# Reload tables in two buffers, a gated-attention branch begun three steps earlier, and a product block held behind the third pair of heads

## The chip, the cores and the metric

The kernel runs on one core of a Trainium2 chip. The metric is device time in microseconds (us), the median of several executions. All data are float32. The core has TensorE (PE, matrix products; its weight loads are listed apart as PEld), VectorE (DVE), ScalarE (ACT), GpSimd (POOL) and SyncE (SP), which here issues nearly all DMAs in one queue, in program order. Each engine runs its own instructions in a fixed order and waits on semaphores for the others.

## The reference

An encoder of two layers over 256 tokens of width 1024. Each layer is a half-step SwiGLU feed-forward block, a mixer and a second feed-forward block; the mixer is what the change touches:

```
h = RMSNorm(x)
u | q k v gate zf zb | aq ak av = split(h @ w_in)
y_s5   = S5(u)        # complex diagonal state space, both directions; gelu; y * sigmoid(y @ w_glu)
y_gla  = GLA(q,k,v,zf,zb): 4 heads, gated linear attention both ways,
         per-head RMSNorm, then * silu(gate)
y_attn = attention: 8 query heads, 2 key heads of 64, rotary, softmax
gates  = sigmoid(h @ w_merge_gate + b)       # 3 x 1024 columns
x += (gates0*(y_s5@w_s5) + gates1*(y_gla@w_gla) + gates2*(y_attn@w_attn)) @ w_out
```

## The kernel before, in words

**Dense products.** Every weight matrix is streamed once. `load` (L204) brings 128 x 2 x 512 blocks (512 KB) into a ring of five raw buffers, ScalarE rounds each into `hi` (L224), VectorE subtracts to get `lo` (L225), and `mm3` makes three products of 512 columns per pair of k-row and token tile (L234 to L236). A step of `stream` (L238) takes four k-rows, so 24 products. An optional `held` instruction makes the products of a block stand behind that instruction in the order (`behind`, L196); it is an ordering edge on TensorE's own queue and no semaphore.

**The mixer** (L671) is a main chain of steps into which three side generators are woven by `weave` (L94). The main chain is the input projection (blocks listed from L716, two steps each, the first two blocks together as steps 0 to 3, 14 steps in all) and then the parts of `MAIN` (L42): the three gate streams g0 to g2 (four steps each), `S` (what is left of S5), `G` (S5's GLU), `b0` (branch of S5), `L` (rest of GLA), `b10` (first half of GLA's branch), `A` (rest of attention), `b11`, `b20`, `b21`, and then the output product. `RATES` (L41) gives for S5, GLA and attention, in this order, the main step from which the generator is advanced and how many of its own steps it advances per main step. S5 has 34 own steps, GLA 27 (three for its gates, then six for each head), attention 19 (seven for norm and rotary, then three for each of four pairs of heads). What `weave` sets is the order in which instructions are emitted, with a priority for the sides; from it a planner with a cost model of its own fixes each engine's order of instructions and the hand-over of buffers.

**S5** (L778) runs in four quarters. For each quarter it needs tables that were computed ahead, during the feed-forward blocks, by `s5_tables` (L515): `bb` and `cc` (512 KB each), `e` (768 KB: 512 KB of turn factors and, behind them, 256 KB of decay factors `rr`), and `mt` (128 KB). Quarters 1 to 3 are stored to scratch memory (`scr`) and loaded back; quarter 0 stays where it was computed, and is the last to be computed. In a quarter: 8 products S from `bb` (L816; the trace has each as two passes), four VectorE products of `e` with S and two sums, four scans with `rr` (L833, L834), four more products of `e` with the scans' results, and 48 small products yp from `mt` and `cc` (L851, L854). `s5_tiles` (L770) has one buffer for each table, and all four loads stand at the head of the quarter that uses them, so that a load waits until the quarter before has used its table for the last time.

**GLA** (L921) computes its gate logits `lg` and decays for all heads, and then for each head cumulative sums, scores `sp`, states `kv`, output `go`, the norm and the product with the swish gate `gs`, and a transposition `goT`. `gs` is made by `ev_g` (L706) when the gate block of the input projection is complete. **Attention** (L1018) has for each pair of heads the scores `as` (L1068), a softmax, transpositions `apt` (L1083) and the products `ao` (L1090); then `split_into` makes hi and lo of the result. `self.last_ao` is the last `ao` product issued, and `b11` is held behind it (L736). S, yp, lg, sp, kv, go, as and ao all take PSUM tiles from one ring of three buffers (`psm`, L137).

Of the kernel before, what the change touches and what calls it, by code (L numbers as in the profile page):

```python
# [15 lines left out]
P = 128  # L16
# [12 lines left out]
NQ = 4  # L29
# [10 lines left out]
PREP = ((2, 1.8), (6, 0.85))  # L40
RATES = (3, 2.5, 10, 2.0, 14, 1.75)  # L41
MAIN = "g0 g1 g2 S G b0 L b10 A b11 b20 b21"  # L42
# [6 lines left out]
SCR_BB, SCR_CC, SCR_E, SCR_R, SCR_M, SCR = 0, 1024, 2048, 3072, 3584, 3840  # L49
SCR_AT = {"bb": (SCR_BB, SCR_CC), "e": (SCR_E, SCR_M), "cc": (SCR_CC, SCR_E), "mt": (SCR_M, SCR)}  # L50

# [74 lines left out]
class Enc:  # L126
# [388 lines left out]
    def s5_tables(self, l, pp):  # L515
# [38 lines left out]
        for q in (1, 2, 3, 0):  # L554
# [31 lines left out]
            for i in range(2):  # L586
                for a in range(4):
                    for d in range(2):
# [9 lines left out]
            v.scalar_tensor_tensor(ks[:, :, 3], dm, dcol, kp[0][:, :, 0], op0=ALU.mult, op1=ALU.add)  # L598
            E = ld["e"][:, :SCR_R - SCR_E].rearrange("p (r g c) -> p r g c", r=2, g=GQ)
            f8 = [self.ef[:, i, gs].unsqueeze(2).to_broadcast((P, GQ, 8, 8)) for i in range(2)]  # L600
# [3 lines left out]
            yield from self.cmul_steps(e8[0], e8[1], f8[0], f8[1], g8[0], g8[1], tt)  # L604
            nc.gpsimd.tensor_tensor(ld["e"][:, SCR_R - SCR_E:].rearrange("p (g c) -> p g c", g=GQ),
                                    self.r4[:, gs].unsqueeze(2).to_broadcast((P, GQ, 64)),
                                    self.tab(C_RM, 64).unsqueeze(1).to_broadcast((P, GQ, 64)), op=ALU.mult)
            scr = self.scr[l, q]
            if q:
                for name in ("bb", "cc", "e"):  # L610
                    a, z = SCR_AT[name]
                    nc.sync.dma_start(scr[:, a:z], ld[name])
# [58 lines left out]
    def mixer(self, l, nm, nxt):  # L671
        nc = self.nc
        with self.tc.tile_pool(name=f"mx{l}", bufs=1) as mp:
# [32 lines left out]
            def ev_g(t, ps):  # L706
# [13 lines left out]
                (cols((w, c(1024, 1536))), 512, ev_tr(m["kT"])),  # L720
                (cols((w, c(1536, 2048))), 512, self.evac_scaled(lambda t: m["v"][:, t], rstd)),
                (cols((w, c(2592, 3104))), 512,
                 self.evac_scaled(lambda t: m["qk"][:, t, 0:8].rearrange("p h d -> p (h d)"), rstd)),
                (cols((w, c(2048, 2560))), 512, ev_g),
            ]
# [43 lines left out]

    def s5_tiles(self):  # L770
        return {name: self.ld.tile([P, z - a], F32, name=self.nm(name), tag="s5" + name) for name, (a, z) in SCR_AT.items()}

# [5 lines left out]
    def s5(self, l, m):  # L778
# [20 lines left out]
        yield  # L799
        yg = mp.tile([P, 2, 4, 8, 16], F32, name=f"yg{l}", tag="yg")  # L800
        for q in range(NQ):
            if q:
                ld = self.s5_tiles()
                self.s5_load(l, q, ld, "bb", "e", "cc", "mt")
            else:
                ld = self.ahead.pop(l)
            bb = ld["bb"].rearrange("p (a r m) -> p a r m", a=4, r=2)
            e = ld["e"][:, :1024].rearrange("p (r c) -> p r c", r=2)
            rr = ld["e"][:, 1024:]
            cc = ld["cc"].rearrange("p (r g f) -> p r g f", r=2, g=GQ)  # L810
# [3 lines left out]
            for r in range(2):  # L814
                for a in range(4):
                    nc.tensor.matmul(S[r][:, a].rearrange("p g c -> p (g c)"), bb[:, a, r],  # L816
                                     U[:, pair[a]].rearrange("p g c -> p (g c)"), start=True, stop=True)
            yield
            t1, t2, t3, t4 = (self.t2([P, 512]) for _ in range(4))
# [12 lines left out]
            for i, V in ((0, t1), (1, t3)):  # L832
                nc.vector.tensor_tensor_scan(run[:64, i, 1:], rr[:64, :511], V[:64, :511], 0.0, op0=ALU.mult, op1=ALU.add)  # L833
                nc.vector.tensor_tensor_scan(run[64:, i, 510::-1], rr[64:, 511:0:-1], V[64:, 511:0:-1], 0.0,  # L834
                                             op0=ALU.mult, op1=ALU.add)
            nc.vector.memset(edge[:64, :, :, 0:1], 0.0)
            nc.vector.memset(edge[64:, :, :, 63:64], 0.0)
# [8 lines left out]
            for i in range(2):  # L846
                gh = [(g, h, h * 2 + i, yp[g][h * 64:(h + 1) * 64, i].rearrange("p t f -> p (t f)"))
                      for g in range(2) for h in range(2)]
                for g, h, a, o in gh:
                    rows = slice(g * 64, g * 64 + 64)  # L850
                    nc.tensor.matmul(o, U[rows, pair[a], g], mt[rows, a], start=True, stop=False)  # L851
                for r, X in enumerate((X0, X1)):
                    for g, h, a, o in gh:
                        nc.tensor.matmul(o, X[:, g * 4 + a], cc[:, r, g * 4 + a], start=False, stop=r == 1)  # L854
            for g in range(2):
                o = yg[:, q // 2].rearrange("p t (k i e) f -> p k e i t f", k=2, i=2)[:, q % 2, g]
                nc.scalar.copy(o, yp[g])
# [160 lines left out]
    def attn(self, l, m, y):  # L1018
# [44 lines left out]
        for j in range(4):  # L1063
# [24 lines left out]
            for s in range(NT):  # L1088
                for v in range(2):
                    self.last_ao = nc.tensor.matmul(po[v * 64:(v + 1) * 64], m["av"][:, s, (j // 2) * 64:(j // 2 + 1) * 64], PT[v][:, s],  # L1090
                                     start=s == 0, stop=s == NT - 1)
            self.split_into(yh[:, j], yl[:, j], po)
            yield
# [180 lines left out]
```

## Time and profile before

| | |
|---|---|
| median of 3 runs | 1330.19 us (1330.01 to 1330.89) |
| profiled execution | 1329.67 us, its span 1327.9 us |
| TensorE busy | 1295.5 us, 98% of the span; weight loads 79% |
| VectorE busy | 1000.0 us, 75% |
| ScalarE busy | 699.2 us, 53% |
| DMA | 249.87 MB, mean 188 GB/s |
| granted TensorE clock | 0.999 |

The two mixers lie at about 213 to 456 us and 868 to 1111 us of the span. Busy time of TensorE counts products that are under way, and these overlap; idle time is what is left between them. A row of a timeline gives the start, the duration, the engine and what it does, and in brackets how long the engine had been idle before it and which instruction ended that.

### The profile page before, as it was taken

How to read it: one execution, taken by the hardware profiler on the slowest of the kernel's cores; microseconds unless marked ns; L12 is line 12 of the kernel's file. 1: busy time of each engine (PE TensorE's matmuls, PEld its weight loads, DVE VectorE, ACT ScalarE, POOL GpSimd, SP SyncE). 2: the span in 40 equal slices, each digit the busy share in tenths (PEclk: the TensorE clock that was granted, in tenths of full speed). 3: DMA queues.
4: the chain of work that ended last, by engine and by line, in shares of the span. 5: the costliest groups of instructions: out<-in, count | busy, mean ns of one | idle time of the engine just before them, and what ended most of it. 6: DMA issues, size and time to landing. Idle time of an engine off the chain costs nothing.

```text
span 1327.9 us, 19275 instructions
## 1 busy us (share of the span) xinstructions
PE 1295.5 (98%) x6792; PEld 1049.2 (79%) x6792; DVE 1000.0 (75%) x1798; ACT 699.2 (53%) x1132; POOL 86.7 (7%) x109
## 2 busy tenths in 40 slices
PE   8999999999999999999999999999999999999997
PEld 6788778878787788788888778887787868888886
DVE  5899996789997678998576767557899966655553
ACT  6454455547676455554454454454485854645442
POOL 1022221000100000202010000000001000000000
PEclk9999999999999999999999999999999999999999
DMA  8775686775463367677656665566655625555661
GB/s 258 181 212 165 227 298 195 203 240 193 145 206 112 112 191 176 187 232 258 200 163 207 194 210 189 171 189 208 209 193 182 183 76 162 175 175 186 195 205 63
DMA packets 201264, 249.87 MB, mean 188 GB/s; under 512 B 40920, under 2 KB 134664, under 8 KB 201168
## 3 DMA queue, kind: packets, MB, share of 16 engines
q1 hardware_dynamic: 200416, 247.33, 59.8%
q10 hardware_dynamic: 752, 1.32, 0.3%
q8 instruction: 53, 0.87, 0.3%
q14 instruction: 43, 0.35, 0.1%
HBM read 234.44 MB, written 13.11 MB: 186 GB/s over the span
## 4 chain that ended last, share of the span: by engine, by line
PE 78%; DVE 10%; DMA 5%; issue 3%; ACT 1%; SPq 1%; POOL 0%; POOLq 0%; DVEq 0%; ACTq 0%
PE mm L234 23%; PE mm L235 23%; PE mm L236 23%; DVE lo L225 3%; DVE t L335 2%; DMA e<-scr 2%; DMA raw<-in_ffn_w_up 1%; PE st L304 1%; DVE run L834 1%; PE ao L1090 1%; SPq L220 1%; ACT hi L224 1%; PE S L816 1%; DVE run L833 1%; PE as L1068 1%
## 5 line engine op out<-in xcount | busy, mean ns | idle before, releaser
L225 DVE TENSOR_TENSOR lo<-raw,hi 128x1024 fp32r<-128x1024 f32 (+2 forms) x414 | 498.2, 1208 | 200.0 <-ACT hi L224 192.2
L224 ACT CAST hi<-raw 128x1024 fp32r<-128x1024 f32 (+2 forms) x414 | 428.6, 1039 | 340.3 <-PE mm L236 259.6
L235 PE MATMUL mm<-lo,hTh 128*128 128x512 f32 (+1 forms) x1120 | 440.0, 394 | 5.1 <-DVE lo L225 4.8
L234 PE MATMUL mm<-hi,hTh 128*128 128x512 f32 (+1 forms) x1120 | 440.2, 395 | 2.4 <-DVE gate L757 1.5
L236 PE MATMUL mm<-hi,hTl 128*128 128x512 f32 (+1 forms) x1120 | 431.4, 392 | 0.0
L235 PEld LDWEIGHTS mm<-lo,hTh 128*128 128x128 f32 x1120 | 211.0, 188 | 47.7 <-DVE lo L225 7.6
L234 PEld LDWEIGHTS mm<-hi,hTh 128*128 128x128 f32 x1120 | 211.0, 189 | 45.3 <-DVE gate L757 2.4
L236 PEld LDWEIGHTS mm<-hi,hTl 128*128 128x128 f32 x1120 | 210.5, 189 | 40.7
L235 PE MATMUL mm<-lo,sThffn 128*128 128x512 f32 x352 | 137.6, 392 | 1.2 <-DVE lo L225 1.2
L236 PE MATMUL mm<-hi,sTlffn 128*128 128x512 f32 x352 | 137.6, 392 | 0.0
L234 PE MATMUL mm<-hi,sThffn 128*128 128x512 f32 x352 | 136.2, 393 | 0.6 <-ACT hi L224 0.6
L235 PEld LDWEIGHTS mm<-lo,sThffn 128*128 128x128 f32 x352 | 66.1, 188 | 15.7 <-DVE lo L225 2.2
L234 PEld LDWEIGHTS mm<-hi,sThffn 128*128 128x128 f32 x352 | 66.1, 188 | 14.5 <-ACT hi L224 1.1
L236 PEld LDWEIGHTS mm<-hi,sTlffn 128*128 128x128 f32 x352 | 66.1, 188 | 14.0
L300 ACT ACTIVATE t<-mm,rstd 128x256 f32<-128x256 f32 x88 | 41.0, 473 | 54.6 <-PE mm L236 52.5
L306 ACT CAST sThffn<-st 128x256 fp32r<-128x256 f32 x88 | 31.5, 372 | 67.5 <-PE st L304 67.0
L307 DVE TENSOR_TENSOR sTlffn<-st,sThffn 128x256 fp32r<-128x256 f32 x88 | 35.7, 417 | 32.6 <-ACT sThffn L306 32.5
L301 DVE SCALAR_TENSOR_TENSOR t<-mm,rstd,t 128x256 f32<-128x256 f32 x88 | 40.9, 477 | 10.2 <-ACT t L300 10.0
L615 POOL COPY kx<-ks 128x128 f32<-128x128 f32 x32 | 28.1, 917 | 230.4 <-DVE ks L598 187.0
L304 PE MATMUL st<-ident,t 128*128 128x128 f32 x176 | 31.9, 274 | 0.4 <-DVE t L301 0.3
L304 PEld LDWEIGHTS st<-ident,t 128*128 128x128 f32 x176 | 23.5, 140 | 10.6 <-DVE t L301 0.7
L335 DVE TENSOR_TENSOR t<-e,S 128x512 f32<-128x512 f32 x32 | 20.3, 681 | 13.9 <-DMA e<-scr 11.2
(355 smaller groups left out, 1419.2 us busy)
## 6 DMA issues: line engine op xcount, KB each, us to landing
raw<-in_ffn_w_down SPq DMA_DIRECT2D x88, 512.0 KB, 4.7
raw<-in_ffn_w_gate SPq DMA_DIRECT2D x174, 256.0 KB, 2.9
raw<-in_ffn_w_up SPq DMA_DIRECT2D x174, 256.0 KB, 4.2
raw<-in_w_in SPq DMA_DIRECT2D x48, 512.0 KB, 4.9
raw<-in_w_merge_gate SPq DMA_DIRECT2D x48, 512.0 KB, 4.5
raw<-in_w_out SPq DMA_DIRECT2D x16, 512.0 KB, 3.9
scr<-e SPq DMA_DIRECT2D x6, 768.0 KB, 6.9
e<-scr SPq DMA_DIRECT2D x6, 768.0 KB, 6.0
```

Source lines behind the costliest of these rows:

```text
L224: nc.scalar.copy(hi[:, j:z, :width], raw[:, j:z, :width])
L225: nc.vector.tensor_tensor(lo[:, j:z, :width], raw[:, j:z, :width], hi[:, j:z, :width].bitcast(F32), op=ALU.subtract)
L234: return (nc.tensor.matmul(ps, act[0], w[0], start=first, stop=False), nc.tensor.matmul(ps, act[0], w[1], start=False, stop=False), nc.ten ...
L235: nc.tensor.matmul(ps, act[0], w[1], start=False, stop=False),
L236: nc.tensor.matmul(ps, act[1], w[0], start=False, stop=last))
L300: nc.scalar.activation(sg, ps[:, :256], AF.Silu, scale=rstd[:, t:t + 1])
L301: nc.vector.scalar_tensor_tensor(s, ps[:, 256:], rstd[:, t:t + 1], sg, op0=ALU.mult, op1=ALU.mult)
L304: nc.tensor.transpose(pt[:, j], s[:, j * P:(j + 1) * P], self.ident)
L306: nc.scalar.copy(h, pt)
L307: nc.vector.tensor_tensor(sl[:, 2 * b:2 * b + 2, t * P:(t + 1) * P], pt, h.bitcast(F32), op=ALU.subtract)
L335: self.nc.vector.tensor_tensor(out, a, b, op=ALU.mult)
L615: nc.gpsimd.tensor_copy(kx[:, :, s], ks.rearrange("p g j f -> p g (j f)")[:, :, (3 - s) * 16:(3 - s) * 16 + 64])
```

## The change

The `e` table is cut into `e` (turn factors, 512 KB) and `r` (decay factors, 256 KB), and `e` gets two buffers, here and where the tables are computed. The loads for quarter q+1 are no longer at its head: `bb` and `e` are loaded behind the products S of quarter q, `r` behind its scans, `cc` and `mt` behind its products yp. GLA begins at main step 7 in place of 10, at 1.8 own steps per main step in place of 2.0; the gate block of the input projection changes place with the block of attention's q and is now steps 10 and 11 instead of 12 and 13. `last_ao` is set by the third pair of heads (j = 2) instead of the fourth, and so `b11` is held behind that one.

```
-RATES = (3, 2.5, 10, 2.0, 14, 1.75)
+RATES = (3, 2.5, 7, 1.8, 14, 1.75)
-SCR_AT = {"bb": (SCR_BB, SCR_CC), "e": (SCR_E, SCR_M), "cc": (SCR_CC, SCR_E), "mt": (SCR_M, SCR)}
+SCR_AT = {"bb": (SCR_BB, SCR_CC), "e": (SCR_E, SCR_R), "r": (SCR_R, SCR_M), "cc": (SCR_CC, SCR_E), "mt": (SCR_M, SCR)}
+SCR_BUFS = {"e": 2}
...
-                for name in ("bb", "cc", "e"):
+                for name in ("bb", "cc", "e", "r"):
...
                 (cols((w, c(1536, 2048))), 512, self.evac_scaled(lambda t: m["v"][:, t], rstd)),
+                (cols((w, c(2048, 2560))), 512, ev_g),
                 (cols((w, c(2592, 3104))), 512,
                  self.evac_scaled(lambda t: m["qk"][:, t, 0:8].rearrange("p h d -> p (h d)"), rstd)),
-                (cols((w, c(2048, 2560))), 512, ev_g),
...
-    def s5_tiles(self):
-        return {name: self.ld.tile([P, z - a], F32, name=self.nm(name), tag="s5" + name) for name, (a, z) in SCR_AT.items()}
+    def s5_tiles(self, *names):
+        return {name: self.ld.tile([P, z - a], F32, name=self.nm(name), tag="s5" + name, bufs=SCR_BUFS.get(name, 1))
+                for name, (a, z) in SCR_AT.items() if not names or name in names}
...
+        ahead = self.ahead.pop(l)
         for q in range(NQ):
-            if q:
-                ld = self.s5_tiles()
-                self.s5_load(l, q, ld, "bb", "e", "cc", "mt")
-            else:
-                ld = self.ahead.pop(l)
+            ld = ahead
...
                     nc.tensor.matmul(S[r][:, a].rearrange("p g c -> p (g c)"), bb[:, a, r],
                                      U[:, pair[a]].rearrange("p g c -> p (g c)"), start=True, stop=True)
+            if q + 1 < NQ:
+                ahead = self.s5_tiles("bb", "e")
+                self.s5_load(l, q + 1, ahead, "bb", "e")
             yield
...
                 nc.vector.tensor_tensor_scan(run[64:, i, 510::-1], rr[64:, 511:0:-1], V[64:, 511:0:-1], 0.0,
                                              op0=ALU.mult, op1=ALU.add)
+            if q + 1 < NQ:
+                ahead.update(self.s5_tiles("r"))
+                self.s5_load(l, q + 1, ahead, "r")
...
                         nc.tensor.matmul(o, X[:, g * 4 + a], cc[:, r, g * 4 + a], start=False, stop=r == 1)
+            if q + 1 < NQ:
+                ahead.update(self.s5_tiles("cc", "mt"))
+                self.s5_load(l, q + 1, ahead, "cc", "mt")
...
-                    self.last_ao = nc.tensor.matmul(po[v * 64:(v + 1) * 64], m["av"][:, s, (j // 2) * 64:(j // 2 + 1) * 64], PT[v][:, s],
+                    ao = nc.tensor.matmul(po[v * 64:(v + 1) * 64], m["av"][:, s, (j // 2) * 64:(j // 2 + 1) * 64], PT[v][:, s],
                                      start=s == 0, stop=s == NT - 1)
+            if j == 2:
+                self.last_ao = ao
```

## Rows read from the trace of the kernel before

**Rows 1.** The page, part 1: busy us (share of the span) and instructions.

```profile
PE 1295.5 (98%) x6792; PEld 1049.2 (79%) x6792; DVE 1000.0 (75%) x1798; ACT 699.2 (53%) x1132; POOL 86.7 (7%) x109
```

**Rows 2.** Busy time by stretch: first mixer, a feed-forward stretch (640:660), second mixer.

```profile
core 0: us, PE busy (x) PEld busy (x) DVE busy (x) ACT busy (x) POOL busy (x), PEclk, DMA share, GB/s
246.00:300.00 54.00, 52.21 (x330) 41.73 (x329) 45.68 (x59) 21.96 (x31) 0.54 (x2) 1.00 0.66 215
340.00:362.00 22.00, 19.55 (x94) 15.25 (x93) 21.24 (x34) 10.43 (x23) 2.25 (x2) 1.00 0.54 168
420.00:439.00 19.00, 16.67 (x90) 10.11 (x89) 13.03 (x31) 11.14 (x34) 0.69 (x1) 1.00 0.10 34
640.00:660.00 20.00, 20.00 (x94) 16.61 (x94) 11.44 (x14) 10.21 (x15) 0.00 (x0) 1.00 0.58 186
901.00:955.00 54.00, 52.27 (x330) 41.77 (x329) 45.73 (x59) 22.21 (x31) 0.54 (x2) 1.00 0.65 216
995.00:1017.00 22.00, 19.58 (x94) 15.20 (x93) 21.39 (x35) 10.67 (x23) 2.52 (x2) 1.00 0.54 168
1075.00:1094.00 19.00, 16.67 (x90) 10.39 (x90) 12.69 (x30) 10.71 (x34) 0.69 (x1) 1.00 0.11 31
```

**Rows 3.** TensorE's waits, whole span: us in total, times, longest us.

```profile
PE S L816 <- DVE t L335: 3.5, 4, 1.1
```

**Rows 4.** VectorE's waits, whole span, same columns.

```profile
DVE t L335 <- DMA e<-scr: 11.2, 4, 3.4
```

**Rows 5.** Timeline of VectorE, first mixer: start us, us, instruction, [idle before <-releaser].

```profile
268.42 1.28 DVE L335 TENSOR_TENSOR t<-e,S 128x512 f32<-128x512 f32 x2 [3.38 <-DMA e<-scr]
...
292.51 1.28 DVE L335 TENSOR_TENSOR t<-e,S 128x512 f32<-128x512 f32 x2 [2.27 <-DMA e<-scr]
```

**Rows 6.** The page, part 6: DMA issues, KB each, median us to landing.

```profile
raw<-in_ffn_w_gate SPq DMA_DIRECT2D x174, 256.0 KB, 2.9
...
e<-scr SPq DMA_DIRECT2D x6, 768.0 KB, 6.0
```

**Rows 7.** Timeline of TensorE, first mixer, 349 to 357 us.

```profile
351.74 0.50 PE L235 MATMUL mm<-lo,hTh 128*128 128x512 f32 x1 [1.54 <-DVE lo L225]
...
355.99 0.50 PE L234 MATMUL mm<-hi,hTh 128*128 128x512 f32 x1 [0.77 <-DVE gate L757]
```

**Rows 8.** VectorE's groups from 296 to 436 us: two of GLA's twelve groups.

```profile
L341 DVE TENSOR_TENSOR la<-t 128x256 f32<-128x256 f32 x8 | 3.1, 414 | 0.0
...
L1005 DVE TENSOR_SCALAR gss<-gss 128x2 f32<-128x2 f32 x4 | 0.7, 163 | 0.0
```

**Rows 9.** Timeline of TensorE, end of attention in the first mixer.

```profile
423.59 1.08 PE L1090 MATMUL ao<-t,av 128*64 128x256 f32 x6 [0.68 <-ACT t L1085]
...
429.77 0.30 PE L1012 MATMUL goT<-ident,t 128*128 128x128 f32 x1 [0.55 <-DVE t L1009]
...
436.91 1.08 PE L1090 MATMUL ao<-t,av 128*64 128x256 f32 x6 [1.08 <-ACT t L1085]
```

**Rows 10.** Timeline of VectorE behind the last pair of heads.

```profile
438.67 0.42 DVE L669 TENSOR_TENSOR yal<-ao,yah 128x256 fp32r<-128x256 f32 x1
```

**Rows 11.** Timeline of TensorE, first mixer: S5's third and fourth quarter, GLA's logits, the GLU.

```profile
297.87 0.64 PE L936 MATMUL lg<-t,wa 96*128 96x256 f32 x4
...
317.27 0.69 PE L854 MATMUL yp<-cc,t 128*64 128x64 f32 x16
...
330.04 1.95 PE L816 MATMUL S<-U,bb 128*128 128x128 f32 x16
...
389.81 0.28 PE L885 MATMUL glu<-ysh,hi 128*128 128x256 f32 x1
```

**Rows 12.** Timeline of VectorE: the split of S5's result.

```profile
386.69 1.28 DVE L669 TENSOR_TENSOR ysl<-yT,ysh 128x512 fp32r<-128x512 f32 x2
```

**Rows 13.** SyncE's queue, its waits over the whole span: us in total, times, longest.

```profile
SPq L220 <- DVE lo L225: 588.8, 242, 15.8
```

**Rows 14.** TensorE's waits from 100 to 213 us, where the tables are computed.

```profile
PE mm L235 <- DVE lo L225: 1.2, 1, 1.2
```

More of the change, by code (lines that the diff above doesn't have):

```diff
@@ L598, in s5_tables @@
             v.scalar_tensor_tensor(ks[:, :, 3], dm, dcol, kp[0][:, :, 0], op0=ALU.mult, op1=ALU.add)
-            E = ld["e"][:, :SCR_R - SCR_E].rearrange("p (r g c) -> p r g c", r=2, g=GQ)
+            E = ld["e"].rearrange("p (r g c) -> p r g c", r=2, g=GQ)
             f8 = [self.ef[:, i, gs].unsqueeze(2).to_broadcast((P, GQ, 8, 8)) for i in range(2)]
@@ L604, in s5_tables @@
             yield from self.cmul_steps(e8[0], e8[1], f8[0], f8[1], g8[0], g8[1], tt)
-            nc.gpsimd.tensor_tensor(ld["e"][:, SCR_R - SCR_E:].rearrange("p (g c) -> p g c", g=GQ),
+            nc.gpsimd.tensor_tensor(ld["r"].rearrange("p (g c) -> p g c", g=GQ),
                                     self.r4[:, gs].unsqueeze(2).to_broadcast((P, GQ, 64)),
@@ L800, in s5 @@
         yg = mp.tile([P, 2, 4, 8, 16], F32, name=f"yg{l}", tag="yg")
+        ahead = self.ahead.pop(l)
         for q in range(NQ):
-            if q:
-                ld = self.s5_tiles()
-                self.s5_load(l, q, ld, "bb", "e", "cc", "mt")
-            else:
-                ld = self.ahead.pop(l)
+            ld = ahead
             bb = ld["bb"].rearrange("p (a r m) -> p a r m", a=4, r=2)
-            e = ld["e"][:, :1024].rearrange("p (r c) -> p r c", r=2)
-            rr = ld["e"][:, 1024:]
+            e = ld["e"].rearrange("p (r c) -> p r c", r=2)
+            rr = ld["r"]
             cc = ld["cc"].rearrange("p (r g f) -> p r g f", r=2, g=GQ)
```

## The prediction

> **What bounds the kernel now.** I read the busy times of the page first, then a table of stretches, then the waits of TensorE and VectorE, then timelines around each wait. TensorE is busy for 98% of the span [rows 1], so time can come back only where it idles, or where it does needless work, and the change takes away no product. The table of stretches [rows 2] shows where it idles. In a feed-forward stretch it is busy for 20.00 of 20.00 us. In the first mixer it idles 54.00 - 52.21 = 1.79 us between 246 and 300, 22.00 - 19.55 = 2.45 us between 340 and 362, and 19.00 - 16.67 = 2.33 us between 420 and 439; in the second mixer, in the same places, 1.73, 2.42 and 2.33 us. These six add up to 13.05 us. That is what the change can get at; the rest of the idle time lies in the first loads, the table computation and the end, outside it.
>
> The three places have three causes. The first: the products S wait for VectorE, which still has to read the S tiles of the quarter before (3.5 us in four waits [rows 3]), and VectorE itself stands still for the load of `e` (11.2 us in four waits [rows 4]), twice per mixer [rows 5]. The second: VectorE is full, 21.24 of 22.00 us [rows 2], and two runs of products wait for it, 1.54 us for a `lo` and 0.77 us for an evacuation of a gate [rows 7]. The third: at the end of attention nothing dense is left to put between the short steps; TensorE waits 0.68, 0.55 and 1.08 us for ScalarE and VectorE to finish a softmax or a norm [rows 9].
>
> **The tables in two buffers.** Before, the load of `e` could start only when VectorE had used the old table for the last time, and it takes 6.0 us to land [rows 6]. With two buffers it is issued a whole quarter earlier; the two starts in [rows 5] are 24.1 us apart, so 512 KB, a part of what took 6.0 us, has landed long before. VectorE no longer waits, the S tiles come free in time, and the 3.5 us of [rows 3] go. I take -3.5 us. What is late next there is `r`, still in one buffer and loaded behind the scans; a load of 256 KB lands in 2.9 us [rows 6], against a quarter of 24.1 us, or 24.1 - 5.6 = 18.5 us without the waits for `e`. The waits for `bb`, `cc` and `mt` stay as they were: each follows the last use of its one buffer, as before. The bounds of this term are 0 (the S tiles are late for another reason) and -3.5.
>
> The cut of `e` adds three stores and three loads per layer to SyncE's queue. SyncE stands for 588.8 us waiting until VectorE frees a weight buffer [rows 13]; the issues lie in that slack, and I cost them at nothing. Without it a load of weights would come later by one issue, and TensorE has up to five buffers of 12 products each in hand. Where the tables are computed, `e` has a second buffer too, and VectorE's order there may come out otherwise; TensorE's longest wait for it there is 1.2 us [rows 14]. I take 0, with bounds of -1.2 and +1.2.
>
> **GLA from step 7.** A main step has 24 products, and TensorE starts 94 instructions in 20.00 us at full rate [rows 2], 0.21 us each, so three steps are at least 15 us, in which 3 x 1.8 = 5.4 of GLA's 27 own steps now run. GLA's work on VectorE is twelve groups from 3.1 us down to 0.7 us [rows 8], together 27.3 us, so 5.4 steps carry 5.5 us. VectorE idles 54.00 - 45.68 = 8.3 us between 246 and 300 [rows 2], so there is room for it where it goes, and as much goes out of the full stretch at 340. The lower rate, 1.8 for 2.0, makes GLA end at step 7 + 27/1.8 = 22.0 instead of 10 + 27/2.0 = 23.5, so the tail gets part of it too.
>
> In the full stretch the two mixers lose 2.45 + 2.42 = 4.87 us. VectorE stays near full there, since S5, GLA and attention still overlap, and the order is a planner's; I take half, -2.4, with bounds of -4.9 (all of it) and +4.9 (the same loss again). In the tail the waits of 0.68 and 0.55 us stand because the last head of GLA runs beside the last pairs of heads, and `b10`, which needs that head, can't fill them [rows 9]. A head that ends 1.5 steps sooner (at least 7.6 us) lets the 24 products of `b10`, 5.1 us, lie in between: -2 x 1.23 = -2.5, bounds 0 and -2.5. Against this I set a new cost: between 246 and 300 VectorE will now be about as full as at 340, where it cost 2.4 us per mixer. I charge half of that, +2.4 in all, bounds 0 and +4.9.
>
> The gate block goes two steps forward and q two steps back. Attention begins at step 14 and q is complete at the end of step 13, so no wait is added in that order; both blocks have the same shape and loads. I cost it at 0.
>
> **The held block.** `b11` has 24 products, 5.1 us. Before they stood behind the last pair of heads, where TensorE idled 1.08 us for ScalarE's copy [rows 9]; now they may fill that gap: -2 x 1.08 = -2.2, bounds 0 and -2.2. The cover that goes: behind the last `ao` (its end is 436.91 + 1.08 = 437.99) the split of the last pair ran until 439.09 [rows 10] while `b11` kept TensorE busy. Now `b20` follows, and its first 12 products need only pairs 0 and 1: 2.5 us against 1.1 us of split. Without that cover it would cost 2 x 1.1 = +2.2.
>
> **The sum.** -3.5 - 2.4 - 2.5 + 2.4 - 2.2 = -8.2 us. Against the profiled execution's 1329.67 us (span 1327.9 and 1.8 around it) that is 1321.5; the median of the runs is 0.5 us above that execution, so 1322.
>
> **The rivals.** First, *the stall only moves*: the stretch at 340 stays as it is and the tail too, and only the loads and the held block pay, while the new stall is paid: -3.5 - 2.2 + 2.4 = -3.3, so 1326.9. For it: the planner's order fits its own costs, and the waits at 340 look like a mismatch of them, which a shift doesn't cure. Against: VectorE's total is 75% [rows 1], so there is room for all of it.
>
> Second, *hidden anyway*: the S tiles come from a ring of three, and if the wait of [rows 3] is handed to the next user of the ring, and what the tail gains is lost again in front of the output product, nothing changes: 1330. For it: VectorE's wait of 11.2 us [rows 4] cost TensorE only 3.5 us [rows 3]. Against: the wait of 1.08 us in [rows 9] has no other work near it at all.
>
> Third, on the other side, *the ring of three makes S5 late*. In [rows 11] the third quarter's yp end at 317.27 + 0.69 = 317.96, and the fourth quarter's S start at 330.04, 12.1 us later, after GLA's logits have entered the ring at 297.87. Begun three steps sooner, GLA meets one quarter more. If that one waits 12.1 us too, S5 gains 11.2 / 2 = 5.6 us from the loads and has 389.81 - (386.69 + 1.28) = 1.8 us to spare before the GLU [rows 11, 12]; the GLU comes 12.1 - 5.6 - 1.8 = 4.7 us late in each mixer. It decides from 7.4 us of added waiting on. With -3.5 and -2.2 kept: +9.4 - 5.7 = +3.7, so 1334. Against it: emission order puts S5's steps ahead of GLA's in the same main step, and TensorE would have parts of GLA and attention to do.
>
> Fourth, *more comes back than the idle time*. At 640 weight loads are busy 16.61 of 20.00 us, 83%; at that share the 41.73 us of loads between 246 and 300 would take 50.3 us and not 54.00, 3.7 less, and the six stretches together 28.1 us less, where idle time is 13.05 [rows 2]. If the dense products now spread between the short ones give this back in the same proportion, the gain is 8.2 x 28.1 / 13.05 = 17.7 us, so 1312.5. I hold it unlikely, since the short products (64 rows or columns) are as many as before and load less. [...]
>
> **How the numbers follow.** Forecast as summed 0.55 (its own range 1318 to 1327), the stall moves 0.17, hidden anyway 0.11, S5 late 0.11, more than the idle time 0.06. What can be told from no change is about 0.2%, 2.7 us, so faster is below 1327.5 and slower above 1332.9. Faster: 0.55 + 0.06 + 0.10 of the second case, which ends near that line, 0.71. Same: 0.07 + 0.11 = 0.18. Slower: 0.11. The range from 1315 to 1330 takes in the forecast with most of its bounds, the stall that moves and most of "hidden"; it leaves out S5 late and most of the last case.
>
> **What would show it.** Right: no wait of VectorE for `e`, none of S for VectorE; GLA's first logits near 280 instead of 297.87; its last `goT` well before the third pair's `ao`; products of `b11` before the fourth pair's `ao`; idle time in the six stretches near 5 us in place of 13.05. Wrong: S of the third or fourth quarter waiting behind GLA's tiles with the GLU later than the gate streams' last product; a wait for `lo` between 270 and 330 as long as that of [rows 7]; or idle time gone and the span unchanged, which would mean that TensorE's work itself got slower.

## The result, and the profile after

The kernel after takes 1349.18 us (median; 1347.42 to 1354.16), before 1330.1; the ratio is 1.015, 95% interval 1.0126 to 1.0174. The forecast was 1322 us, faster, in a range up to 1330. Its profiled execution took 1347.42 us with a span of 1345.6, 17.7 us more than before. Where the 17.7 us lie is read by counting: both traces hold the same 4896 dense products (`mm`) in nearly the same order, and the n-th of them starts later by so much more than at the stretch before:

```
first feed-forward with tables   +5.9        second with tables   +3.3
first mixer                      +4.1        second mixer         +4.2        anywhere else 0.0
```

Page part 1 of the kernel after, against [rows 1]:

```profile
PE 1302.8 (97%) x6792; PEld 1053.0 (78%) x6792; DVE 1000.0 (74%) x1798; ACT 699.5 (52%) x1132; POOL 95.9 (7%) x109
```

The products are as many, yet TensorE is busy 7.3 us longer, so some of them ran slower; GpSimd is busy 9.2 us longer with the same 109 instructions. Stretches of the kernel after, columns as in [rows 2] (each later than there by what came before it; the fourth reaches over most of the tail, the first and the last lie where the tables are computed):

```profile
200.00:215.00 15.00, 11.98 (x90) 9.26 (x91) 8.60 (x13) 5.12 (x9) 1.12 (x4) 0.89 0.68 209
252.00:306.00 54.00, 54.00 (x342) 43.78 (x341) 47.60 (x65) 33.11 (x49) 0.54 (x2) 1.00 0.61 197
346.00:368.00 22.00, 21.71 (x120) 18.16 (x118) 21.29 (x35) 12.87 (x26) 0.70 (x1) 1.00 0.52 171
400.00:445.00 45.00, 40.37 (x199) 28.67 (x198) 30.19 (x61) 24.55 (x62) 1.40 (x2) 0.96 0.33 99
562.00:575.00 13.00, 10.51 (x40) 7.63 (x39) 12.02 (x33) 3.88 (x8) 7.15 (x16) 0.87 0.50 156
```

Two things are to be seen. The idle time that the forecast went for is gone where S5 and GLA overlap: TensorE fills 54.00 of 54.00 us (before 52.21), and 21.71 of 22.00 (before 19.55). And the column PEclk, 1.00 in all rows of before, is below 1 in three rows: the granted clock was at 0.5 (1.2 GHz) for 3.41 us within each, at 210.6, 429.0 and 569.0 us, and once more at 1091.2, in the second tail. (In the last 5 us of the span it falls in every kernel, before too.) TensorE's waits in the kernel after, whole span, columns as in [rows 3]:

```profile
PE ao L1099 <- ACT t L1094: 5.4, 8, 0.7
PE mm L237 <- DVE lo L227: 5.3, 6, 1.9
PE apt L1092 <- DVE t L1088: 3.3, 4, 0.9
PE kp L593 <- DVE cc L359: 3.0, 1, 3.0
```

The wait of S for VectorE [rows 3] is gone, as is VectorE's for `e` [rows 4]. In their place stand waits of attention's short steps (`ao`, `apt`) and one of 3.0 us in the table computation.

### The profile page after: what moved, and what is told of

It is laid out like the page before. It is cut to its first block, busy times and chain, and to the rows that moved or that the text cites. A ratio compares the mean times of both kernels' runs of the same rounds, so it can differ in the third digit from the quotient of the medians.

```text
span 1345.6 us, 19282 instructions
## 1 busy us (share of the span) xinstructions
PE 1302.8 (97%) x6792; PEld 1053.0 (78%) x6792; DVE 1000.0 (74%) x1798; ACT 699.5 (52%) x1132; POOL 95.9 (7%) x109
## 4 chain that ended last, share of the span: by engine, by line
PE 70%; DVE 13%; DMA 6%; issue 3%; POOL 3%; ACT 2%; SPq 2%; POOLq 0%; ACTq 0%; DVEq 0%
PE mm L236 21%; PE mm L238 20%; PE mm L237 20%; DVE lo L227 4%; DMA raw<-in_ffn_w_up 2%; POOL kx L617 1%; PE st L306 1%; ACT hi L226 1%; PE S L816 1%; DMA scr<-r 1%; SPq L222 1%; DVE t L337 1%; PE as L1077 1%; PE ao L1099 1%; PE apt L1092 1%
## 5 line engine op out<-in xcount | busy, mean ns | idle before, releaser
L617 POOL COPY kx<-ks 128x128 f32<-128x128 f32 x32 | 38.3, 1239 | 252.4 <-DVE ks L600 181.0
L303 DVE SCALAR_TENSOR_TENSOR t<-mm,rstd,t 128x256 f32<-128x256 f32 x88 | 40.9, 477 | 10.6 <-ACT t L302 10.4
L760 ACT ACTIVATE gate<-gate 128x512 f32<-128x512 f32 x24 | 15.2, 633 | 27.5 <-DVE gate L759 27.2
```

Source lines behind the costliest of these rows:

```text
L303: nc.vector.scalar_tensor_tensor(s, ps[:, 256:], rstd[:, t:t + 1], sg, op0=ALU.mult, op1=ALU.mult)
L617: nc.gpsimd.tensor_copy(kx[:, :, s], ks.rearrange("p g j f -> p g (j f)")[:, :, (3 - s) * 16:(3 - s) * 16 + 64])
L760: nc.scalar.activation(g, g, AF.Tanh, scale=0.5)
```

## The experiments

Each kernel is told by its difference to the kernel before, or to another named. The lateness behind each (us, against the profiled execution of before) is at the ends of the first stretch with tables, the first mixer, the second stretch with tables and the second mixer, each for itself:

```
                                 median    ratio [95% interval]       tables  mixer  tables  mixer
after                            1349.18   1.015  [1.0126, 1.0174]     +5.9   +4.1   +3.3   +4.2
e1_held_only                     1331.85   1.0    [0.9982, 1.0019]     +0.5   +1.7   -1.2   +1.4
e2_tables_gla                    1353.06   1.0163 [1.0136, 1.0191]     +7.4   +6.6   +1.5   +8.2
e3_tables_only                   1339.58   1.0061 [1.0039, 1.0082]     +6.1   -0.2   +1.0    0.0
e4_gla_only                      1345.08   1.0112 [1.0082, 1.0142]     +2.1   +8.5   +0.2   +9.1
e5_gla_slow_rate                 1337.08   1.0059 [1.0042, 1.0076]     +0.2   +1.7   -1.0   +1.6
e6_gla_old_rate                  1342.02   1.0091 [1.0075, 1.0108]     +1.2   +6.9   -1.0   +7.1
e7_ao_other_ring                 1353.62   1.0182 [1.0163, 1.0200]     +4.1  +12.0   -0.8  +11.8
e8_swap_only                     1333.69   1.0024 [1.0011, 1.0037]     +4.4   +0.6   -0.4   +2.8
e9_gla_fast_attn                 1355.90   1.0185 [1.0158, 1.0212]     +0.3  +13.1   -0.8  +15.2
e10_attn_early                   1356.15   1.0205 [1.0171, 1.0239]     -0.7  +12.9   -1.1  +13.2
e11_tables_copy_on_act           1333.35   1.0018 [1.0007, 1.0030]     -0.4   -0.3   +4.4    0.0
e12_tables_one_turn_buffer       1339.07   1.0062 [1.0043, 1.0082]     +4.8   -0.3   +1.2   +0.2
e13_gla_b10_behind_pair0         1343.45   1.0102 [1.0081, 1.0124]     +1.0   +7.0   -0.3   +9.8
e14_gla_b10_behind_pair1         1341.78   1.0089 [1.0073, 1.0105]     -0.9   +6.5   -0.2   +7.5
e15_tables_copy_on_act_l0        1333.03   1.0019 [1.0009, 1.0029]     +1.7   +0.2   +1.2   -0.1
e16_tables_l0_b10_behind         1332.95   1.002  [1.0011, 1.0029]     +0.5   -0.1   +3.8    0.0
e17_gla_last_head_back           1328.23   0.9991 [0.9979, 1.0002]     +1.7    0.0    0.0    0.0
e18_tables_l0_last_head_back     1329.24   0.9994 [0.9983, 1.0006]     +1.2   -1.8   +2.4   -1.6
```

One profiled execution need not be the median one (that of e4 is the slowest of its four, that of e5 the fastest); the lateness says where, the ratio how much.

### The three parts apart: e1 to e4

**e1** takes the held block alone, **e3** the tables alone, **e4** GLA's start and the two blocks alone, **e2** the last two together:

```diff
 # e1, in attn
-                    self.last_ao = nc.tensor.matmul(po[...
+                    ao = nc.tensor.matmul(po[...
+            if j == 2:
+                self.last_ao = ao
 # e4
-RATES = (3, 2.5, 10, 2.0, 14, 1.75)
+RATES = (3, 2.5, 7, 1.8, 14, 1.75)
 # and the block of ev_g ahead of that of q; e3: all other hunks; e2: e3 and e4
```

> The kernel before with only the held block moved (b11 behind the third pair of heads). Theory 1 (idle time counted in the trace after): the held block costs what stands idle behind the fourth pair, 0.68 + 0.46 + 0.55 + 1.06 = 2.75 us against 0.40 before, so 2.35 us per mixer: 1330.1 + 4.7 = 1335. Rival A (the whole loss of the tails, 8.2 us per mixer, is the held block's): 1346. Rival B (the held block alone fills the gap of 1.08 us, as predicted, and the tail is lost through GLA's earlier start): 1328. The tables are untouched, so the stretches 0:213 and 460:868 are as before in all three.

> The changed kernel with the held block put back behind the fourth pair. Theory 1: 1349.2 - 4.7 = 1344.5; the clock still falls in both tails, since the idle time at 425 to 432 lies ahead of the held block. Rival A: 1349.2 - 16.4 = 1333. Rival B: 1349 or a little more.

> Only the tables: e and r apart, e in two buffers, loads ahead; GLA from step 10, held block behind the fourth pair. Theory 1: the stretches where the tables are computed lose what they lost in the changed kernel, 5.9 and 3.3 us, and the mixers gain the 3.5 us of S waiting: 1330.1 + 9.2 - 3.5 = 1336; one fall of the clock in each of these stretches, none in the tails. Rival C (the loss in the table stretches is due to other orders of the planner that need all three parts): 1326.5, no fall of the clock.

> Only GLA from step 7 at 1.8 and the gate block ahead of q. Theory 1: no change where the tables are computed; the tails carry what the held block doesn't explain, about 8.2 - 2.4 = 5.8 us per mixer, less what the emptier stretch at 340 gives back (0 to 2.4 per mixer): 1337 to 1342. Rival A (the tails are the held block's): 1325 to 1330. My prediction's own step for this part gave 1330.1 - 2.4 - 2.5 + 2.4 = 1327.6.

The GLA part costs 1.1% (15 us), the tables part 0.6% (8 us), the held block nothing that can be told; the two together 1.6%, so they add up. With the held block on top (the kernel after) the ratio is 1.015, inside the interval of e2.

### The order of GLA and attention: e5 to e10

A first theory was that with 1.8 steps from step 7 GLA's last head enters the PSUM ring of three between the first pair's `ao` and the second pair's scores, and that this ring holds attention up.

```diff
-RATES = (3, 2.5, 10, 2.0, 14, 1.75)
+RATES = (3, 2.5, 7, 1.55, 14, 1.75)   # e5, blocks swapped
+RATES = (3, 2.5, 7, 2.0, 14, 1.75)    # e6, blocks swapped
+RATES = (3, 2.5, 7, 1.8, 14, 2.2)     # e9, blocks swapped
+RATES = (3, 2.5, 10, 2.0, 13, 1.75)   # e10, blocks as before
 # e7: e4 and
-            po = self.psm.tile([P, SEQ], F32, name=self.nm("ao"), tag="sm")
+            po = self.ptr.tile([P, SEQ], F32, name=self.nm("ao"), tag="tr")
 # e8: the swap of the two blocks alone
```

> The GLA part alone (start at step 7, gate block ahead of q), but at 1.55 steps of GLA per main step in place of 1.8; this makes the order in which tiles enter the PSUM ring of three near the pairs of heads that of before: the last head's sp behind the third pair's scores. Theory 1 (with 1.8 the last head's sp and kv enter the ring between the first pair's ao and the second pair's scores, so these scores wait for that ao, and the pairs come one behind the other with no dense products left): second pair's scores back near 409 us, tails as before, 1327 to 1333 us. Rival A (an earlier start by itself fills VectorE and sends dense products ahead, whatever the order in the ring): near the GLA part alone, 1340 to 1346. Rival B (the swap of the two blocks delays attention): 1340 or more.

> The GLA part alone with the rate of before, 2.0, and the start at step 7: the last head then enters the ring wholly ahead of the second pair of heads. Theory 1 (order in the ring): no score waits for an ao of the pair before, 1326 to 1334 us. Rival A (earlier start itself): 1342 to 1350, the more so since more of GLA is early. Rival B (swap): 1340 or more.

> The GLA part alone with 1.8 from step 7, but the attention output ao in the PSUM ring of the transposes (two buffers) in place of the ring of three. Theory 1: the second pair's scores no longer wait for the first pair's ao; they come at 409 to 414 us in place of 420, and 7 to 14 us come back: 1331 to 1338. Rival A and B: 1343 to 1347, the same tail.

> Only the gate block put ahead of q; GLA from step 10 at 2.0 as before. Theory 1 and rival A: 1329 to 1333, no change. Rival B (q's block two steps later delays the attention's norms and with them the pairs): 1338 to 1346.

The first theory fell with e7: `ao` left the ring, and the second pair's scores started at 423.7 us all the same. (That it was slower than e4 says little: its longest waits, 2.74 and 2.28 us, are of the transpositions `apt`, whose two buffers `ao` now shares.) e6, with `sp`, `kv` and `go` of the last head ahead of the second pair, was slow too, where the theory gave 1326 to 1334. e5, with the last head behind the third pair's scores, lost only 1.7 us per mixer in its profiled execution, 1332.13 us, but its median is 5 us higher, between what the theory (1327 to 1333) and rival A (1340 to 1346) gave. e8 lost 0.6 and 2.8 us in the mixers; most of its lateness is in the first stretch, which the swap doesn't touch (below). That rules out the swap as the cause of e4's 15 us.

> The GLA part alone (start at step 7, 1.8 steps, gate block ahead of q), with attention at 2.2 of its own steps per main step in place of 1.75, so that the first two pairs of heads are ahead of GLA's last head in the order. Theory 2 (attention's four pairs are the longer chain; the order of the change puts GLA's last head in front of the second pair, and what is left behind it is pairs alone, one behind the other): second pair's scores at 405 to 411 us, last ao at 436 to 440, tail as before, 1327 to 1335 us. Rival A (the earlier start itself, by what it takes from VectorE): 1341 to 1347 as with the GLA part alone.

> The kernel before with one change that the kernel after doesn't have: attention from step 13 in place of 14, GLA as before. Theory 2 (attention is the chain that ends the mixer): faster than before by 1 to 4 us per mixer, 1322 to 1328. Rival A (VectorE and not the order is what counts; it gets no less to do): 1329 to 1333. A third reading (VectorE is overfull at 340 to 362 and attention's norms now fall into it): 1334 to 1340.

Theory 2, that attention is the longer chain and wants to be earlier, failed in both, which are 25 us slower than before: e9 and e10 are the slowest of all. In e9 the second pair's scores came at 406.26 us, as forecast, but its last `ao` at 447.64 and not at 436 to 440. In e10 the loss begins where attention's transposes now stand ahead of the GLU in TensorE's order (timeline of TensorE in e10):

```profile
389.76 0.66 PE L1055 MATMUL aqp<-ident,qk 128*128 128x128 f32 x4 [1.27 <-ACT yT L866]
390.69 0.44 PE L1059 MATMUL akp<-ident,t 128*128 128x128 f32 x2 [0.28 <-ACT yT L866]
391.71 0.50 PE L885 MATMUL glu<-ysh,hi 128*128 128x256 f32 x2 [0.57 <-ACT ysh L668]
392.93 0.38 PE L886 MATMUL glu<-ysl,hi 128*128 128x256 f32 x1 [0.72 <-DVE ysl L669]
```

Four waits in a row, 2.84 us, and at 393.9 the granted clock fell to 0.5 for 3.41 us. A table of TensorE's time in the first mixer, from one dense product to another, the same two in each run (at 257 and 479 us in the kernel before), says what the lost time is made of. "At 0.5" is the time at a granted clock of 0.5; at most half of it is lost:

```
           in all    idle    at 0.5                   in all    idle    at 0.5
before     221.6      7.2      0.0          e9         234.7    13.0     17.1
after      225.8      9.8      3.4          e10        234.6    12.8      6.8
e4         230.2     11.5     10.2          e13        228.7    10.8      6.8
e5         223.3      8.7      0.0          e14        228.2     9.5     10.2
e6         228.5      8.7     10.2          e17        221.7     6.6      3.4
e7         233.7     12.3     17.1          e3         221.4     4.1      3.4
```

Of e4's 8.6 us here, 4.3 are idle time; half of 10.2 us at half clock, 5.1, covers the rest (some of that time is idle as well). In e10 the two leave some 4 us of its 13.0 open.

### The tables: e11, e12, e15

In the kernel after, TensorE stands still for 3.02 us at 208 us. The chain behind it, in three of its engines (timelines of TensorE, GpSimd and SyncE, kernel after):

```profile
211.06 0.58 PE L593 MATMUL kp<-cc,bb 64*32 64x96 f32 x16 [3.02 <-DVE cc L359]
...
187.83 11.83 POOL L617 COPY kx<-ks 128x128 f32<-128x128 f32 x4 [28.42 <-DMA e<-scr]
...
199.68 3.61 SPq L620 DMA_DIRECT2D scr<-kx  x8
203.39 0.39 SPq L222 DMA_DIRECT2D raw<-in_ffn_w_down  x1
```

and the same place in the kernel before:

```profile
186.67 2.12 POOL L615 COPY kx<-ks 128x128 f32<-128x128 f32 x4 [1.37 <-DVE ks L598]
...
189.08 3.74 SPq L618 DMA_DIRECT2D scr<-kx  x8
192.92 0.39 SPq L220 DMA_DIRECT2D raw<-in_ffn_w_down  x1
```

Four small copies take 11.83 us in place of 2.12 (three take 0.3 us, one 11.1); their stores are issued 10.6 us later, and a load of weights stands behind them in SyncE's queue, issued at 203.39 in place of 192.92. The `lo` made from it, and VectorE's `cc` behind that, are late, and TensorE's `kp` waits. Two edits test it:

```diff
 # e11: e3 and
-                nc.gpsimd.tensor_copy(kx[:, :, s], ...
+                nc.scalar.copy(kx[:, :, s], ...
 # e15: e3 and
+                (nc.gpsimd.tensor_copy if l else nc.scalar.copy)(kx[:, :, s], ...
 # e12: e3, and in s5_tables one e and r for all four quarters
+        er = self.s5_tiles("e", "r")
         for q in (1, 2, 3, 0):
-            ld = self.s5_tiles()
+            ld = self.s5_tiles("bb", "cc", "mt")
+            ld.update(er)
```

> The tables part alone, with the four small copies kx of a quarter on ScalarE in place of GpSimd. Theory 2 (a copy on GpSimd stands for up to 11 us beside VectorE's runs of operations with two inputs in SBUF, and its stores hold the next load of weights on SyncE's queue; that is the 3 us of idle and the clock's fall near 208 us): the first table stretch ends 4 to 6 us sooner than with the tables part alone, 1332 to 1335 us. Rival A (the delay there is VectorE's own, cc in front of kp): the stretch stays late, 1338 to 1341.

> The tables part alone, but where the tables are computed one buffer of e and r serves all four quarters, as before; the mixers keep both buffers and the early loads. Theory 2 (the second buffer lets VectorE and GpSimd run ahead in the computation and that makes the harm there): the first table stretch as before, 1330 to 1334 us. Rival A (the cut of e into e and r, with more stores in SyncE's queue, makes it): the stretch stays 4 to 6 us late, 1337 to 1341.

> The tables part alone, with the kx copies on ScalarE for layer 0 only and on GpSimd for layer 1, where they stood for at most 4 us. Theory (the starved GpSimd copy is all of the tables part's harm in layer 0, and ScalarE's copies are what made layer 1 late in the run with both layers on ScalarE): 1328 to 1331 us. Rival (the second layer's stretch is late whatever is done to kx, by its own idle time and the fall of the clock behind it): 1332 to 1335.

e11: the first stretch is on time again (-0.4 against +6.1 us). Where the chain above runs, between the products that start at 195 and at 213 us in the kernel before, e3 loses 4.8 us and e11 none; so the slow copy was the main part of the loss. The other 1.7 us come back earlier, where e11 also moves copies of 5.4 and 4.2 us that the kernel before has too. e12 refutes the second buffer as the cause of the slow copy: with one buffer it is as slow, and the time is what its rival, the cut of `e` itself, gave. GpSimd's copies and VectorE's operation at the moment when the slow copy ends, in e12:

```profile
186.70 11.82 POOL L619 COPY kx<-ks 128x128 f32<-128x128 f32 x4 [28.50 <-DMA raw<-in_ffn_w_down]
...
198.05 0.87 DVE L1187 SCALAR_TENSOR_TENSOR hTl<-pt,vecT,hTh 128x256 fp32r<-128x256 f32 x2
```

From 187.15 to 198.05 VectorE runs back to back operations with two tensors from SBUF (`bb`, `T`, `lo`, `cc`); then comes one whose main input `pt` is in PSUM, and the copy that began at 187.17 ends with it, at 198.29. The Trainium skill, "SBUF — State Buffer", section "Who interferes with whom", says that a VectorE instruction with two SBUF inputs contends with a GpSimd instruction that reads SBUF, over a shared pair of ports that is an exclusive lock. The trace of e12 agrees that the copy stood, and there it got through only behind VectorE's whole run, after 11.1 us, and not behind one instruction. But VectorE has the same operations in the same order in the kernel before (timeline of VectorE, the first of the run and what ends it):

```profile
187.13 0.28 DVE L355 TENSOR_TENSOR bb<-T,T 128x128 f32<-128x128 f32 x1
...
198.21 0.86 DVE L1174 SCALAR_TENSOR_TENSOR hTl<-pt,vecT,hTh 128x256 fp32r<-128x256 f32 x2
```

There the four copies beside them took 2.12 us. At this place the third copy took 11.1 us in all four profiled executions with the cut table and the copies on GpSimd (after, e2, e3, e12), and 0.4 us in all twelve with the old table. How the cut brings that about is not shown.

e15's theory failed in part: the second stretch with tables is +1.2 there, but e16 below, with the same copies, has +3.8 and a fall of the clock at 559.6, so what made e11 late in its second layer was not ScalarE's copies. e15 stays 0.19% slower than before; it loses 4.5 us ahead of 107 us, where the clock falls too, and regains 2.8 by 208. What does that was not pursued.

### What covers the tail: e13, e14, e16, e17, e18

```diff
 # e13 (j == 0) and e14 (j == 1): e4 and (with self.last_ao for ao); e16 (j == 0): e15 and
-            gens["b10"] = lambda: self.branch(l, 1, y, gates, (0,))
+            gens["b10"] = lambda: self.branch(l, 1, y, gates, (0,), held=self.first_ao)
+            if j == 0:
+                self.first_ao = ao
 # e17: e4 and, in gla; e18: e15, e4 and
         for h in range(GH):
+            for _ in range(3 if h == 3 else 0):
+                yield
```

> The GLA part alone (1345.1, tails of both mixers 8 to 10 us late), with all 24 products of b10 put behind the first pair's ao, so that they lie between the steps of the later pairs. Theory 3 (the tail is bare: idle steps between the pairs' short products, and the clock falls because of them): no fall of the clock in the tails, idle time in a tail down from 4 to 5 us to 2, 1333 to 1338 us. Rival C (the chain through the softmax steps sets the end, whatever TensorE does between): last ao as late as before, 1342 to 1348. Rival D (idle time only moves ahead of the first pair's ao, where nothing dense is left then): 1340 to 1350 with idle time at 412 to 420.

> As the run before, with b10 behind the second pair's ao. Theory 3: like it or a little later, 1333 to 1340, as the last two pairs get all of the cover and the second none. Rival C: 1342 to 1348. Rival D: more idle time at 412 to 432 than in the run before and so slower than it, 1345 to 1355.

> The run before and b10 held behind the first pair's ao as well; GLA from step 10 as before. Theory 3 (dense products kept for the tail cover the three waits of 0.55 to 1.09 us there): 1 to 2 us per mixer less than the run before, 1325 to 1329. Rival D (idle time moves ahead of the first ao): 1330 to 1336.

Theory 3 got 0.7 and 2 us of idle time in the first mixer, and the clock fell in the tails all the same. The products went out in one block behind the pair that held them (16 from 415.6 us in e13, 22 from 423.4 in e14) and not between the steps: the waits of 0.5 to 1.0 us stayed. In e16 nothing moved; its mixers are those of e15.

> The GLA part alone (1345.1; start at step 7, 1.8 steps), with three empty steps ahead of the last head, so that its sp, kv and go stand in the order where they stood before: sp behind the second pair's scores, kv and go behind the third's. Theory 4 (the last head is what lies between the short steps of the pairs; moved ahead it leaves them alone, idle and at half clock): idle time in the first mixer back to 7 to 8 us, no fall of the clock in the tails, 1328 to 1334 us. Rival A (an earlier start by itself): 1341 to 1347 with the same tails. Rival C (the chain of pairs is late for another reason): second pair's scores still at 418 to 422, 1338 to 1346.

> The tables part with the kx copies of layer 0 on ScalarE, and the GLA part with the last head back in its place; held block as before. Theory 4: both harms are gone, 1326 to 1332 us. Rival A or C: the tails' loss stays, 1340 to 1348.

e17 differs from e4 by three empty steps ahead of GLA's last head, and is 17 us faster, 0.9991 [0.9979, 1.0002] of before. The two run alike up to the first pair's `ao`. Timeline of TensorE in e4 (without the dense products, and one row of its stretch):

```profile
409.55 0.65 PE L1090 MATMUL ao<-t,av 128*64 128x256 f32 x2
410.12 1.16 PE L982 MATMUL sp<-t,t 128*128 128x128 f32 x8
...
418.77 1.08 PE L1090 MATMUL ao<-t,av 128*64 128x256 f32 x6
...
420.20 0.70 PE L1068 MATMUL as<-akT,aqT 64*128 64x256 f32 x2
...
424.37 0.81 PE L1083 MATMUL apt<-ident,t 128*128 128x128 f32 x4 [0.90 <-DVE t L1079]
425.85 0.65 PE L1090 MATMUL ao<-t,av 128*64 128x256 f32 x2 [0.68 <-ACT t L1085]
426.43 2.19 PE L1068 MATMUL as<-akT,aqT 64*128 64x256 f32 x8
...
433.42 0.72 PE L1083 MATMUL apt<-ident,t 128*128 128x128 f32 x4 [0.61 <-DVE t L1079]
434.81 0.65 PE L1090 MATMUL ao<-t,av 128*64 128x256 f32 x2 [0.68 <-ACT t L1085]
...
443.25 0.72 PE L1083 MATMUL apt<-ident,t 128*128 128x128 f32 x4 [0.96 <-DVE t L1079]
444.65 1.97 PE L1090 MATMUL ao<-t,av 128*64 128x256 f32 x6 [0.67 <-ACT t L1085]
...
418.00:446.00 28.00, 21.35 (x102) 12.75 (x100) 15.38 (x37) 13.49 (x42) 0.70 (x1) 0.91 0.19 59
```

and in e17:

```profile
409.53 0.65 PE L1092 MATMUL ao<-t,av 128*64 128x256 f32 x2
410.10 1.14 PE L1070 MATMUL as<-akT,aqT 64*128 64x256 f32 x8
...
418.72 1.08 PE L1092 MATMUL ao<-t,av 128*64 128x256 f32 x6
419.72 0.94 PE L984 MATMUL sp<-t,t 128*128 128x128 f32 x6
...
421.77 0.65 PE L1092 MATMUL ao<-t,av 128*64 128x256 f32 x2 [0.45 <-ACT t L1087]
422.40 1.42 PE L1070 MATMUL as<-akT,aqT 64*128 64x256 f32 x8
...
425.30 1.08 PE L1092 MATMUL ao<-t,av 128*64 128x256 f32 x6 [0.68 <-ACT t L1087]
426.31 0.71 PE L993 MATMUL kv<-v,la 128*128 128x128 f32 x4
...
431.48 0.30 PE L1014 MATMUL goT<-ident,t 128*128 128x128 f32 x1 [0.55 <-DVE t L1011]
...
438.63 1.08 PE L1092 MATMUL ao<-t,av 128*64 128x256 f32 x6 [1.09 <-ACT t L1087]
...
418.00:440.00 22.00, 19.21 (x106) 11.97 (x105) 13.81 (x34) 12.77 (x40) 0.69 (x1) 1.00 0.17 54
```

At 410.1 us e17 runs the second pair's scores `as`, e4 the last head's `sp`; e4's scores come at 420.20. Behind them e4 has the steps of three pairs with hardly anything beside them, and ten waits that add up to 6.65 us; e17 has four, 2.77 us, since `sp`, `kv` and `go` of the last head lie between the pairs. The clock is 1.00 in e17's tail and 0.91 over e4's 28 us; the eight scores that take 1.14 us in e17 take 2.19 at half clock in e4. The last `ao` comes at 444.65 against 438.63, 6.0 us, and the 24 products of `b11` behind it take 7.7 us against 5.6: 8.1 us in all, of the 8.5 by which the two mixers differ.

So theory 4 holds, and the rival that GLA's earlier start costs the time by itself falls, since e17 keeps that start. e17 brings two things at once, the second pair's scores 10 us sooner and the last head as cover. On the first alone e9 says something (timeline of TensorE in e9):

```profile
406.26 2.09 PE L1068 MATMUL as<-akT,aqT 64*128 64x256 f32 x8
...
425.78 1.16 PE L982 MATMUL sp<-t,t 128*128 128x128 f32 x8
...
446.15 0.82 PE L1083 MATMUL apt<-ident,t 128*128 128x128 f32 x4 [1.36 <-DVE t L1079]
447.64 1.97 PE L1090 MATMUL ao<-t,av 128*64 128x256 f32 x6 [0.68 <-ACT t L1085]
```

Its second pair's scores come sooner than those of e17, but its last head lies ahead of the third pair, and the steps of the last two pairs stand alone again, with six waits from 432 us on, 4.95 us in all, and two falls of the clock (436.4 and 446.6 us). So early scores of the second pair don't save the tail by themselves; whether the head as cover alone would is not tested. e18 joins e17's edit with the mended tables: its mixers gain 1.8 and 1.6 us, its table stretches give back 1.2 and 2.4, and 0.9994 [0.9983, 1.0006] can't be told from before. No kernel here beats the one before.

## Why the prediction was wrong

**The step that failed** is the tail: "A head that ends 1.5 steps sooner (at least 7.6 us) lets the 24 products of `b10`, 5.1 us, lie in between: -2 x 1.23 = -2.5, bounds 0 and -2.5." The rows [rows 9] show two waits beside a GLA head and were read as waits that the head causes. The head was their cover; with it gone, waits of that kind came at nearly every step. Nor do products of `b10` lie in between when they are ready: only 6 of the 24 need the last head, and the other 18 go out in one block ahead of it (from 414.6 us in e4). The term was bounded at 0 above; the mixers of e4 lost 8.5 and 9.1 us. And the head ends less early than the 7.6 us of the term. Its rows in the kernel after, first logits and last transposition, where everything in the first mixer is 5.9 us late from the tables on:

```profile
282.13 0.87 PE L945 MATMUL lg<-t,wa 96*128 96x256 f32 x6
...
431.58 0.63 PE L1021 MATMUL goT<-ident,t 128*128 128x128 f32 x2
```

With these 5.9 us taken off, the logits start 21.7 us sooner than at 297.87 [rows 11], the third head's `kv` 8.9 us sooner (396.0 against 399.0) and the last `goT` 4.1 us sooner than at 429.77 [rows 9].

**The tables' preparation**, "I take 0, with bounds of -1.2 and +1.2", was the second error: 0.6%, some 8 us. The bounds came from one row [rows 14], a wait of VectorE's `lo`; the chain that grew runs through GpSimd and SyncE, and the forecast weighed SyncE's slack as a sum [rows 13], when what counts is which load stands behind the stores at that moment.

**S for VectorE, -3.5**: right as a wait. It is gone, and idle time in the two mixers of e3 is 3.1 and 2.8 us less. The time did not come: the net is -0.2 and 0.0. One fall of the clock takes back up to 1.7 us in each mixer, half of 3.41, but the fall is not all of it: e11, e15 and e16 have these tables and no fall in the first mixer, their idle time there is 2.7 to 2.8 us less, and between the two products of the table above they take between 0.3 us less and 0.2 us more. The rest goes into products that start a little slower with nothing idle between them; why is not shown.

**The full stretch at 340, -2.4, and the new stall, +2.4**: the first was low, from 2.45 to 0.29 us of idle time; the second about right in the first mixer (three waits between 321 and 330 us, 1.74 us). At 385 us the first mixer of the kernel after had gained 3.9 us, what the forecast hoped for. It lost 8.1 behind that.

**The held block, -2.2**: nothing, in e1, whose ratio leaves room for some 2.4 us either way; by the count of products each tail comes out 0.4 us later from 418 and from 1075 us on, and not 1.1 sooner. Its products go ahead of the fourth pair's `ao`, as forecast, but these `ao` then come later (445.18 us in e1 for the last, 436.91 before), and behind them TensorE waits for VectorE's gates instead (0.55 and 1.06 us at 452 and 455 us, before one of 0.40). The clause "now they may fill that gap" left out that on an engine that runs in a fixed order a block of 5 us in a gap of 1 us delays what comes after it by 4.

The rivals were off as well. The one on the slow side, S5 late through the ring of three, came half true: the third quarter's `yp` end at 341.3 us and not at 317.96 [rows 11], 17.5 us later in the mixer, but the GLU, where it saw the cost, starts at 392.5, 3.2 us sooner in the mixer than at 389.81. "Hidden anyway" is what became of the tables' gain, though not by the way it gave. *More comes back than the idle time* found no support: where idle time was filled, as in e3, less came back. No case had a fall of the clock, since no row of before shows a clock below 1.00.

## What to carry to other kernels

A stretch with two short chains side by side and an idle microsecond in it is not a stretch in which one chain is in the other's way: before one is moved, count which steps of the other it stands between, and what would stand there then. Where an engine is full nearly everywhere, moving work earlier earns at most the idle time it fills and pays at the place it came from; e17, with that place left as it was, no longer paid, but came out even with the kernel before and not ahead of it. And a term that touches GpSimd needs the row of each of its instructions, the longest beside the median, and of what waits behind it in a queue.

## What the runs showed of the hardware

**The clock.** Before, it stood at full speed until the last 5 us of the span. In nine kernels (after, e2, e4, e6, e7, e9, e10, e13, e14) it fell in both tails, always to 0.5 and for 3.41 us or a small multiple (6.83, 13.65, 17.07), behind stretches in which TensorE was idle for part of the time and ran short products otherwise: e4's first fall, at 427.1 us, comes behind waits of 0.90 and 0.68 us. Not each such stretch was followed by one: e17's tail has a wait of 1.09 us and keeps the clock, and single falls come elsewhere (in e17 at 272.6 and 927.9 us, beside S5). Where TensorE is the bound, 3.41 us at half clock lose at most half, 1.7 us, about as much as the 1.58 us of idle time in front of that fall.

**GpSimd beside VectorE.** The line of the slow copy in the kernel after, over the table computation (min, median and longest, ns):

```profile
L617 POOL COPY kx<-ks x16: 288/298/11111, 122.7 to 214.6; 128x128 f32<-128x128 f32 x16
```

The same happens without the change: another GpSimd operation, of 1.06 us alone, took 14.02 us in e8,

```profile
172.45 14.02 POOL L605 TENSOR_TENSOR e<-r,tcst 128x512 f32<-128x512 f32 x1 [11.92 <-DMA scr<-e]
```

and 13.8 and 13.9 in e4 and e7, where the run before took 1.52. In these three the first stretch with tables is 2.1 to 4.4 us late though nothing in it is changed; in the others with unchanged tables, where it takes 1.2 to 1.6, it is -0.9 to +1.7. So part of the 3 to 8 us by which runs of one kernel differ here may come from it; that was not tested.
